# A two-layer attention encoder: block sums of the first seven-product group, an earlier weight split, and other banks for one set of transposes

## The chip, the cores and the metric

The kernel runs on one core of a Trainium2 chip. The metric is the device time in microseconds (us) of one execution. Before the change three runs took 1867.33, 1861.46 and 1866.14 us, with a median of 1866.14. A further execution was run under the hardware profiler; all rows below come from it.

## The reference, cut to what matters

The reference is an encoder trunk of two layers in float32, for 512 tokens of 1024 channels. Each layer does

```
h = RMSNorm(x);  four attention mixers, gated, merged
x = x + merged @ W_out                   (1024 x 1024)
hm = RMSNorm(x, mlp_norm_g)
u = square(relu(hm @ W_up))              (1024 x 4096)
x = x + u @ W_down                       (4096 x 1024)
```

The change touches the stretch from the second norm to the first quarter of `hm @ W_up`. It occurs once in each layer.

## The kernel before, in words

Matrix products must be close to float32, so every operand is split in two: `split` (lines 213 to 218) writes `hi`, a rounded copy made by ScalarE (line 215), and `lo`, the rest, made by VectorE (line 216, which waits for `hi`). A product of two operands is then three matmuls on TensorE: hi with hi, hi with lo, lo with hi.

**The order of work.** The program is written as one stream of instructions on tiles taken from pools. The tile framework then fixes one order for each engine at build time: it steps through a model of the run, and whenever an engine is free it takes, of the instructions that its model holds to be ready, an early one of the program. On the chip each engine goes through its fixed list and waits at every instruction for the data and buffers it needs. [...]

**Around the change, once in each layer.** `add_rows` (line 1097) adds `merged @ W_out` to the four token tiles `X[t]` of 128 tokens, and sums their squares on ScalarE (line 317). `norm` (line 324) then goes over the four tiles: eleven small VectorE instructions give the inverse root (`inverse`, lines 331 to 342), two scaled copies (line 349) write the normalised tile `both`, eight transposes on TensorE (line 222) bring it into two PSUM banks of four blocks each, `split` writes `h_hi` and `h_lo` from these banks, and ScalarE copies the banks to `h_raw` (line 361) for later sums. The transposes take their banks from the pool `sps`, which has four. Two more pools hold PSUM: `mm` with three banks, used by `add_rows` just before and by the products after, and `yps` with one.

The 4096 columns of `W_up` are done in four groups `j` of 1024, each of two halves `c` of 512.

- `j = 0, c = 0` is the plain group, `up_first` (line 1153). It loads 1024 x 512 weights as four blocks of 512 KB (`plain_blocks`, line 1136), splits each into `r_hi` and `r_lo` (pools of four buffers), and multiplies them first with tokens 0 to 255 (96 matmuls of 256 columns, which need the first two token tiles only) and then with tokens 256 to 511 (96 more).
- All other halves are done by `up` (line 1195), which needs seven products in place of eight for a 2 x 2 scheme of blocks. `row_sums` (line 1171) makes the sums of activation blocks from `h_raw`. The weight blocks are 512 x 256. One tile `t` starts as block (0,0); after its split for the first product, block (0,1) is added to it, then block (1,1), then block (1,0), with a product after each. Before the change such an addition is an accumulating DMA from HBM issued by GpSimd (`add_block`, line 1123). Another tile, `t3`, is block (0,1) plus block (1,1), added on VectorE (`merge`, line 1133). Each product is 24 matmuls (line 1215).
- From `j = 1` on, the products of `up` alternate with those of `add_product` (line 1325) for `W_down` of the group before.

Raw weights and the tiles `both` share the pool tag `r_raw` (eight buffers). All plain loads are issued by SyncE's queue (SP), in its own fixed order. Line 248 loads the weights of `add_rows`, line 1120 all blocks of `up`, line 321 the gain of the next norm.

Of the kernel before, what the change touches and what calls it, by code (L numbers as in the profile page):

```python
# [10 lines left out]
F32 = mybir.dt.float32  # L11
# [8 lines left out]
P = 128  # L20
S = 512
NT = S // P
D = 1024
# [15 lines left out]
class Weights:  # L39
# [7 lines left out]
    def add(self, layer, name, k0, kk, segs):  # L47
        n = sum(w for _, w in segs)
        off = self.size
        self.units.append((off, layer, name, k0, kk, tuple(segs), n))  # L50
        self.size += P * kk * n
        return off, n
# [45 lines left out]
class Plan:  # L98
# [12 lines left out]
    def take(self, what, n=1):  # L111
        self.free[what] -= n
        assert self.free[what] >= 0, what
# [51 lines left out]
class Net:  # L165
# [158 lines left out]
    def norm(self, pool, X, ms, g, tag="norm_h", bufs=2, keep=None):  # L324

        nc = self.nc
        hi = self.hp.tile([P, KD, S], F32R, name="h_hi", tag="h_hi")
        lo = self.hp.tile([P, KD, S], F32R, name="h_lo", tag="h_lo")
        stt = nc.vector.scalar_tensor_tensor

        def inverse(t):
            small = lambda name: pool.tile([P, 1], F32, name=name, tag=name, bufs=4)
            v, vh, y, w = small("norm_v"), small("norm_vh"), small("norm_y"), small("norm_w")
            nc.vector.tensor_scalar(v, ms[t][0], EPS, None, op0=ALU.add)
            for part in ms[t][1:]:
                nc.vector.tensor_tensor(v, v, part, op=ALU.add)
            nc.vector.tensor_scalar(y.bitcast(I32), v.bitcast(I32), -0.5, RSQRT_MAGIC, op0=ALU.mult, op1=ALU.add)
            nc.vector.tensor_scalar_mul(vh, v, -0.5)
            for _ in range(3):
                stt(w, y, y, vh, op0=ALU.mult, op1=ALU.mult)  # L340
                stt(y, w, 1.5, y, op0=ALU.add, op1=ALU.mult)
            return y

        y = inverse(0)
        for t in range(NT):
            both = pool.tile([P, 2, S], F32, name=tag, tag=tag, bufs=bufs)
            for half in range(2):
                cs = slice(half * S, half * S + S)
                stt(both[:, half, :], X[t][:, cs], y, g[:, cs], op0=ALU.mult, op1=ALU.mult)
            y = inverse(t + 1) if t + 1 < NT else None  # L350
            banks = []
            for half in range(2):
                ps = self.sps.tile([P, 4, P], F32, name="tp", tag="s")
                for j in range(4):
                    self.transpose(ps[:, j, :], both[:, half, j * P:(j + 1) * P])
                self.split(hi[:, half * 4:half * 4 + 4, t * P:(t + 1) * P],
                           lo[:, half * 4:half * 4 + 4, t * P:(t + 1) * P], ps)
                banks.append(ps)
            if keep is not None:
                for half, ps in enumerate(banks):  # L360
                    nc.scalar.copy(keep[half, t // 2][:, :, t % 2 * P:t % 2 * P + P], ps)
        return hi, lo
# [787 lines left out]

        return {(r, t): pool.tile([P, KD // 2, S // 2], F32, name=name, tag="u", bufs=NU) for r in range(2) for t in range(2)}

    def up_first(self, pool, layer, u):

        units = self.plain_blocks(pool, layer, "up", 0, 0)
        tiles = [self.mm.tile([P, S], F32, name="mm", tag="mm") for _ in range(3)]
        tiles.append(self.yps.tile([P, S], F32, name="mm_y", tag="y"))

        early, late = slice(0, S // 2), slice(S // 2, S)
        for f in range(4):  # L1160
            self.fm_group(tiles[f][:, early], self.hT, units, f * P, early)
            self.squared_relu(u[0, 0][:, f, :], tiles[f][:, early])
        for i in range(0, KD, 2):
            for f in range(4):
                for k, hi, lo in units[i:i + 2]:
                    self.mm3(tiles[f][:, late], (hi[:, f * P:f * P + P], lo[:, f * P:f * P + P]),
                             (self.hT[0][:, k, late], self.hT[1][:, k, late]), k == 0, k == KD - 1)
        for f in range(4):
            self.squared_relu(u[0, 1][:, f, :], tiles[f][:, late])
# [22 lines left out]
                self.split(hi[:, i, :], lo[:, i, :], sums[i][:, k, :])  # L1192
        return [own] + [[(hi[:, i, :], lo[:, i, :]) for hi, lo in rest] for i in range(3)]

    def up(self, pool, layer, c0, u, row, sums):


        nc = self.nc
        h, kh, n = S // 2, KD // 2, S // 2
        s1, s2, s3, s4 = sums  # L1200
        part = lambda ks, ts: [tuple(x[:, k, ts] for x in self.hT) for k in ks]
        x11, x12, x22 = (part(range(0, kh), slice(0, h)), part(range(kh, KD), slice(0, h)),
                         part(range(kh, KD), slice(h, S)))
        at = {(r, c): self.W.add(layer, "up", r * kh, kh, [(c0 + n * c, n)])[0] for r in range(2) for c in range(2)}
        load = lambda r, c: self.load_block(pool, at[r, c], kh, n)
        add = lambda raw, r, c: self.add_block(raw, at[r, c], kh, n)
        out = {(t, c): u[row, t][:, 2 * c:2 * c + 2, :] for t in range(2) for c in range(2)}
        bank = lambda: self.mm.tile([P, 2, h], F32, name="mm", tag="mm")

        def product(ps, left, raw, fresh):  # L1210
            right = self.split_block(pool, raw)
            for f in range(2):
                for k, (x, w) in enumerate(zip(left, right)):
                    for i, (a, b) in enumerate(((1, 0), (0, 0), (0, 1))):
                        nc.tensor.matmul(ps[:, f, :], w[a][:, f * P:(f + 1) * P], x[b], start=fresh and f + k + i == 0,  # L1215
                                         stop=k == kh - 1 and i == 2, skip_group_check=True)
                        self.pe(h)

        stt = nc.vector.tensor_tensor
        t = load(0, 0)  # L1220
        a = bank()
        product(a, x11, t, True)
        add(t, 0, 1)
        nc.scalar.copy(out[0, 0], a)
        yield
        c = bank()
        product(c, x12, load(1, 0), True)
        stt(out[0, 0], out[0, 0], c, op=ALU.add)
        self.squared_relu(out[0, 0], out[0, 0])
        yield  # L1230
# [1 line left out]
        product(b, s1, t, True)  # L1232
        add(t, 1, 1)
        nc.scalar.copy(out[1, 1], b)
        t3, w22 = load(0, 1), load(1, 1)
        self.merge(t3, w22)
        yield
        product(b, s4, w22, False)
# [114 lines left out]
    def run(self):  # L1353
# [14 lines left out]
        for layer in range(self.depth):  # L1368
            act = self.attention(layer)
            last = layer == self.depth - 1  # L1370
            with tc.tile_pool(name=f"mlp{layer}", bufs=1) as pool:
# [5 lines left out]
                mine = lambda k, t: tuple(x[:, k, t * P:(t + 1) * P] for x in act)  # L1377
                self.add_rows(pool, X, mine, layer, "out", 0, ms, self.merges)
                raw = self.blocks(pool, "h_raw")
                self.hT = self.norm(pool, X, ms, g, "r_raw", NRIGHT, raw)  # L1380
                if not last:
                    g = self.load_gain(pool, I["attn_norm_g"][layer + 1])
                prev = None
                for j in range(4):
                    u = self.blocks(pool, "u")
                    if j == 0:
                        self.up_first(pool, layer, u)
                        sums = self.row_sums(pool, raw)
                    for c in range(1 if j == 0 else 0, 2):
                        for i, _ in enumerate(self.up(pool, layer, j * D + c * S, u, c, sums)):  # L1390
                            if prev is not None and (i + c) % 2:
                                next(prev, None)
                    if j < 3:
                        prev = self.add_product(pool, X, u, layer, "down", j * KD)
# [89 lines left out]
```

## Time and profile before

| What | us |
|---|---|
| median of three runs | 1866.14 |
| lowest and highest run | 1861.46, 1867.33 |
| the profiled execution | 1864.41 |
| its span (first to last instruction) | 1862.6 |
| TensorE busy | 1772.7 (95%) |
| VectorE busy | 1320.9 (71%) |
| ScalarE busy | 1010.2 (54%) |
| GpSimd busy | 445.2 (24%) |
| mean granted TensorE clock | 0.979 of full speed |

PE stands for TensorE's matmuls, PEld for its weight loads, DVE for VectorE, ACT for ScalarE, POOL for GpSimd, SP for SyncE. PEclk is the clock that TensorE was granted, as a share of full speed; in a row that covers one level only it is either 1.00 (2.4 GHz) or 0.50 (1.2 GHz). In a timeline row the bracket at the end tells how long the engine sat idle before the row, and which instruction ended the wait. Matmuls overlap, so a matmul's duration is longer than the distance to the next one; some matmul records are missing from the trace. The stretch of the change is 588 to 662 us in the first layer and 1503 to 1578 us in the second.

### The profile page before, as it was taken

How to read it: one execution, taken by the hardware profiler on the slowest of the kernel's cores; microseconds unless marked ns; L12 is line 12 of the kernel's file. 1: busy time of each engine (PE TensorE's matmuls, PEld its weight loads, DVE VectorE, ACT ScalarE, POOL GpSimd, SP SyncE). 2: the span in 40 equal slices, each digit the busy share in tenths (PEclk: the TensorE clock that was granted, in tenths of full speed). 3: DMA queues.
4: the chain of work that ended last, by engine and by line, in shares of the span. 5: the costliest groups of instructions: out<-in, count | busy, mean ns of one | idle time of the engine just before them, and what ended most of it. 6: DMA issues, size and time to landing. Idle time of an engine off the chain costs nothing.

```text
span 1862.6 us, 28777 instructions
## 1 busy us (share of the span) xinstructions
PE 1772.7 (95%) x10256; PEld 1577.2 (85%) x10256; DVE 1320.9 (71%) x2645; ACT 1010.2 (54%) x1999; POOL 445.2 (24%) x1245
## 2 busy tenths in 40 slices
PE   6998999999998899999999989999999988999999
PEld 5897887787888899989888879887878888999897
DVE  6677866777655587878567878666876574877872
ACT  4565664455534566566436656645554355656561
POOL 2462254433110011111025504632412001111100
PEclk9998999999999899999999989999999989999999
DMA  4312122121334577878232221222222444878771
GB/s 163 116 53 69 58 80 84 43 69 55 90 91 164 159 179 190 183 194 191 79 105 97 76 60 52 78 72 68 66 66 78 154 145 104 191 192 194 172 178 46
DMA packets 71312, 209.76 MB, mean 113 GB/s; under 512 B 8704, under 2 KB 12288, under 8 KB 71168
## 3 DMA queue, kind: packets, MB, share of 16 engines
q1 hardware_dynamic: 59936, 167.02, 27.5%
q0 software_dynamic: 11232, 40.90, 13.1%
q8 instruction: 80, 1.31, 0.3%
q14 instruction: 64, 0.52, 0.1%
HBM read 203.70 MB, written 4.19 MB: 112 GB/s over the span
## 4 chain that ended last, share of the span: by engine, by line
PE 74%; DVE 8%; POOL 7%; issue 4%; DMA 3%; ACT 2%; SPq 0%; POOLq 0%; DVEq 0%; ACTq 0%
PE mm L1215 14%; PE mm L285 14%; PE mm L286 13%; PE mm L287 13%; PE u L1344 12%; PE tp L222 3%; DMA r_raw<-in_wflat 2%; POOL rs_w_qk L235 2%; PE s L615 2%; POOL rs_w_qk L236 1%; POOL rs_w_qk L237 1%; POOL rs_y_qk L238 1%; PE y L642 1%; PE y L641 1%; DVE w_lo L216 1%
## 5 line engine op out<-in xcount | busy, mean ns | idle before, releaser
L216 DVE TENSOR_TENSOR r_lo<-r_raw,r_hi 128x1024 fp32r<-128x1024 f32 x206 | 250.8, 1221 | 101.1 <-ACT r_hi L215 99.4
L215 ACT CAST r_hi<-r_raw 128x1024 fp32r<-128x1024 f32 x206 | 215.7, 1050 | 128.7 <-PE mm L1215 47.9
L216 DVE TENSOR_TENSOR w_lo<-w_raw,w_hi 128x768 fp32r<-128x768 f32 (+2 forms) x217 | 197.6, 917 | 56.7 <-ACT w_hi L215 54.8
L215 ACT CAST w_hi<-w_raw 128x768 fp32r<-128x768 f32 (+2 forms) x217 | 166.8, 779 | 119.7 <-PE mm L286 76.0
L1125 POOL DMA_DIRECT2D r_raw<-in_wflat x78 | 67.5, 865 | 645.2 <-DVE r_lo L216 641.4
L285 PE MATMUL mm<-h_hi,w_hi 128*128 128x512 f32 x544 | 217.9, 401 | 1.1 <-DVE sig L1040 1.0
L287 PE MATMUL mm<-h_hi,w_lo 128*128 128x512 f32 x544 | 214.4, 400 | 4.4 <-DVE w_lo L216 2.5
L286 PE MATMUL mm<-h_lo,w_hi 128*128 128x512 f32 x544 | 215.7, 397 | 0.0
L286 PE MATMUL mm<-w_lo,h_hi 128*128 128x384 f32 (+1 forms) x576 | 189.8, 331 | 3.4 <-DVE w_lo L216 3.3
L287 PE MATMUL mm<-w_hi,h_lo 128*128 128x384 f32 (+1 forms) x576 | 189.5, 330 | 2.6 <-DVE h_lo L216 2.6
L285 PE MATMUL mm<-w_hi,h_hi 128*128 128x384 f32 (+1 forms) x576 | 187.6, 332 | 1.0 <-ACT w_hi L215 0.5
L235 POOL TENSOR_TENSOR rs_w_qk<-rs_y_qk 128x4 f32<-128x4 f32 (+2 forms) x216 | 66.4, 307 | 415.6 <-DVE rs_y_qk L233 292.0
L1344 PE MATMUL u<-r_lo,l_hi 128*128 128x512 f32 x336 | 132.1, 393 | 0.2 <-DVE r_lo L216 0.2
L1215 PE MATMUL mm<-h_hi,r_lo 128*128 128x256 f32 x448 | 127.2, 284 | 4.8 <-DVE r_lo L216 4.8
L1344 PE MATMUL u<-r_hi,l_lo 128*128 128x512 f32 x336 | 131.6, 392 | 0.0
L1215 PE MATMUL mm<-h_lo,r_hi 128*128 128x256 f32 x448 | 128.2, 286 | 0.0
L1215 PE MATMUL mm<-h_hi,r_hi 128*128 128x256 f32 x448 | 128.0, 286 | 0.0
L1344 PE MATMUL u<-r_hi,l_hi 128*128 128x512 f32 x336 | 126.2, 390 | 0.0
L287 PEld LDWEIGHTS mm<-h_hi,w_lo 128*128 128x128 f32 x544 | 103.3, 190 | 26.8 <-DVE w_lo L216 4.0
L285 PEld LDWEIGHTS mm<-h_hi,w_hi 128*128 128x128 f32 x544 | 103.8, 191 | 23.5 <-DVE sig L1040 2.9
L286 PEld LDWEIGHTS mm<-h_lo,w_hi 128*128 128x128 f32 x544 | 103.5, 190 | 20.5
L286 PEld LDWEIGHTS mm<-w_lo,h_hi 128*128 128x128 f32 x576 | 109.8, 191 | 5.7 <-DVE w_lo L216 4.6
(226 smaller groups left out, 4745.9 us busy)
## 6 DMA issues: line engine op xcount, KB each, us to landing
r_raw<-in_wflat SPq DMA_DIRECT2D x128, 512.0 KB, 4.6
w_raw<-in_wflat SPq DMA_DIRECT2D x168, 384.0 KB, 3.2
r_raw<-in_wflat POOLq DMA_DIRECT2D x78, 512.0 KB, 5.7
w_raw<-in_wflat SPq DMA_DIRECT2D x48, 256.0 KB, 2.6
x<-in_x SPq DMA_DIRECT2D x8, 512.0 KB, 5.6
d_full<-in_mask_d SPq DMA_DIRECT2D x8, 448.0 KB, 4.1
x_save<-x SPq DMA_DIRECT2D x4, 512.0 KB, 2.6
x<-x_save SPq DMA_DIRECT2D x4, 512.0 KB, 4.8
```

The costliest lines, as they stand in the source:

```text
L215: self.nc.scalar.copy(hi, src)
L216: self.nc.vector.tensor_tensor(lo, src, hi.bitcast(F32), op=ALU.subtract)
L222: self.nc.tensor.transpose(out, in_, self.ident_r if short else self.ident)
L235: eng.tensor_tensor(w, y, y, op=ALU.mult)
L236: eng.tensor_tensor(w, w, v, op=ALU.mult)
L285: nc.tensor.matmul(ps, st[0], mv[0], start=first, stop=False)
L286: nc.tensor.matmul(ps, st[0], mv[1], start=False, stop=False)
L287: nc.tensor.matmul(ps, st[1], mv[0], start=False, stop=last)
L615: self.nc.tensor.matmul(ps, q[:, qc], k[:, kc], start=i == 0, stop=i == len(ks) - 1)
L1125: self.nc.gpsimd.dma_start(raw, self.source(off, kk, n), accum_op=ALU.add)
L1215: nc.tensor.matmul(ps[:, f, :], w[a][:, f * P:(f + 1) * P], x[b], start=fresh and f + k + i == 0, stop=k == kh - 1 and i == 2, skip_group_ ...
L1344: nc.tensor.matmul(ps[q], a[:, k, toks], b, start=fresh and k + i == 0, stop=k == len(w) - 1 and i == 2, skip_group_check=True)
```

## The change

Three edits.

1. In the norm ahead of the MLP (the one with `keep`), the transposes of the third token tile (`t == 2`) take their two banks from the pool `mm` in place of `sps`.
2. `plain_blocks` for the plain group (four loads, four splits) stands in the program ahead of the norm, behind `add_rows`. Its result is handed to `up_first`.
3. In the first group (`j == 0`) `up` is called with `alone`: it loads its four weight blocks at once and keeps them, and the three additions to `t` are made by VectorE from the kept blocks (`merge`), where they were accumulating DMAs. The other groups do as before.

```diff
--- before.py
+++ after.py
@@ -350,7 +350,10 @@
             y = inverse(t + 1) if t + 1 < NT else None
             banks = []
             for half in range(2):
-                ps = self.sps.tile([P, 4, P], F32, name="tp", tag="s")
+                if keep is not None and t == 2:
+                    ps = self.mm.tile([P, 4, P], F32, name="tp_mm", tag="mm")
+                else:
+                    ps = self.sps.tile([P, 4, P], F32, name="tp", tag="s")
                 for j in range(4):
                     self.transpose(ps[:, j, :], both[:, half, j * P:(j + 1) * P])
                 self.split(hi[:, half * 4:half * 4 + 4, t * P:(t + 1) * P],
@@ -1150,9 +1153,8 @@
 
         return {(r, t): pool.tile([P, KD // 2, S // 2], F32, name=name, tag="u", bufs=NU) for r in range(2) for t in range(2)}
 
-    def up_first(self, pool, layer, u):
-
-        units = self.plain_blocks(pool, layer, "up", 0, 0)
+    def up_first(self, units, u):
+
         tiles = [self.mm.tile([P, S], F32, name="mm", tag="mm") for _ in range(3)]
         tiles.append(self.yps.tile([P, S], F32, name="mm_y", tag="y"))
 
@@ -1192,7 +1194,8 @@
                 self.split(hi[:, i, :], lo[:, i, :], sums[i][:, k, :])
         return [own] + [[(hi[:, i, :], lo[:, i, :]) for hi, lo in rest] for i in range(3)]
 
-    def up(self, pool, layer, c0, u, row, sums):
+    def up(self, pool, layer, c0, u, row, sums, alone=False):
+
 
 
         nc = self.nc
@@ -1203,7 +1206,15 @@
                          part(range(kh, KD), slice(h, S)))
         at = {(r, c): self.W.add(layer, "up", r * kh, kh, [(c0 + n * c, n)])[0] for r in range(2) for c in range(2)}
         load = lambda r, c: self.load_block(pool, at[r, c], kh, n)
-        add = lambda raw, r, c: self.add_block(raw, at[r, c], kh, n)
+        held = {(r, c): load(r, c) for r, c in ((0, 0), (1, 0), (0, 1), (1, 1))} if alone else {}
+        take = lambda r, c: held[r, c] if alone else load(r, c)
+
+        def add(raw, r, c):
+            if alone:
+                self.merge(raw, held[r, c])
+            else:
+                self.add_block(raw, at[r, c], kh, n)
+
         out = {(t, c): u[row, t][:, 2 * c:2 * c + 2, :] for t in range(2) for c in range(2)}
         bank = lambda: self.mm.tile([P, 2, h], F32, name="mm", tag="mm")
 
@@ -1217,14 +1228,14 @@
                         self.pe(h)
 
         stt = nc.vector.tensor_tensor
-        t = load(0, 0)
+        t = take(0, 0)
         a = bank()
         product(a, x11, t, True)
         add(t, 0, 1)
         nc.scalar.copy(out[0, 0], a)
         yield
         c = bank()
-        product(c, x12, load(1, 0), True)
+        product(c, x12, take(1, 0), True)
         stt(out[0, 0], out[0, 0], c, op=ALU.add)
         self.squared_relu(out[0, 0], out[0, 0])
         yield
@@ -1232,7 +1243,7 @@
         product(b, s1, t, True)
         add(t, 1, 1)
         nc.scalar.copy(out[1, 1], b)
-        t3, w22 = load(0, 1), load(1, 1)
+        t3, w22 = take(0, 1), take(1, 1)
         self.merge(t3, w22)
         yield
         product(b, s4, w22, False)
@@ -1377,6 +1388,7 @@
                 mine = lambda k, t: tuple(x[:, k, t * P:(t + 1) * P] for x in act)
                 self.add_rows(pool, X, mine, layer, "out", 0, ms, self.merges)
                 raw = self.blocks(pool, "h_raw")
+                units = self.plain_blocks(pool, layer, "up", 0, 0)
                 self.hT = self.norm(pool, X, ms, g, "r_raw", NRIGHT, raw)
                 if not last:
                     g = self.load_gain(pool, I["attn_norm_g"][layer + 1])
@@ -1384,10 +1396,10 @@
                 for j in range(4):
                     u = self.blocks(pool, "u")
                     if j == 0:
-                        self.up_first(pool, layer, u)
+                        self.up_first(units, u)
                         sums = self.row_sums(pool, raw)
                     for c in range(1 if j == 0 else 0, 2):
-                        for i, _ in enumerate(self.up(pool, layer, j * D + c * S, u, c, sums)):
+                        for i, _ in enumerate(self.up(pool, layer, j * D + c * S, u, c, sums, j == 0)):
                             if prev is not None and (i + c) % 2:
                                 next(prev, None)
                     if j < 3:
```

## Rows read from the trace of the kernel before

**Rows 1.** The profile's page: busy by engine, chain of waits by engine, accumulating loads
```profile
PE 1772.7 (95%) x10256; PEld 1577.2 (85%) x10256; DVE 1320.9 (71%) x2645; ACT 1010.2 (54%) x1999; POOL 445.2 (24%) x1245
...
PE 74%; DVE 8%; POOL 7%; issue 4%; DMA 3%; ACT 2%; SPq 0%; POOLq 0%; DVEq 0%; ACTq 0%
...
r_raw<-in_wflat POOLq DMA_DIRECT2D x78, 512.0 KB, 5.7
```

**Rows 2.** Busy time by stretch: PE, PEld, DVE, ACT, POOL; PEclk, DMA share, GB/s
```profile
597.00:608.10 11.10, 5.10 (x33) 4.02 (x31) 9.24 (x24) 8.40 (x17) 0.00 (x0) 0.77 0.11 24
608.10:613.20 5.10, 5.10 (x24) 5.10 (x25) 5.00 (x5) 4.25 (x6) 0.00 (x0) 0.50 0.98 349
646.70:650.40 3.70, 3.70 (x17) 3.70 (x18) 2.21 (x2) 1.26 (x3) 0.85 (x1) 0.50 0.53 70
662.00:680.00 18.00, 18.00 (x119) 16.46 (x118) 15.24 (x16) 13.27 (x17) 2.70 (x4) 1.00 0.75 179
1569.70:1574.40 4.70, 4.70 (x22) 4.70 (x23) 2.91 (x3) 2.31 (x3) 0.86 (x1) 0.50 0.83 193
```

**Rows 3.** Timeline of TensorE: start, duration, form, count, idle before and releaser
```profile
600.74 1.33 PE L222 MATMUL tp<-ident,r_raw 128*128 128x128 f32 x8 [1.89 <-ACT h_raw L361]
605.40 1.94 PE L222 MATMUL tp<-ident,r_raw 128*128 128x128 f32 x8 [3.33 <-DVE r_raw L349]
608.10 0.58 PE L285 MATMUL mm<-h_hi,r_hi 128*128 128x256 f32 x1 [0.77 <-ACT r_hi L215]
...
633.29 0.28 PE L1215 MATMUL mm<-h_hi,r_lo 128*128 128x256 f32 x1
633.40 0.28 PE L1215 MATMUL mm<-h_hi,r_hi 128*128 128x256 f32 x1
...
646.69 0.58 PE L1215 MATMUL mm<-w_hi,r_lo 128*128 128x256 f32 x1 [4.71 <-DVE r_lo L216]
655.97 0.38 PE L1215 MATMUL mm<-h_hi,r_lo 128*128 128x256 f32 x1 [1.49 <-DVE r_lo L216]
...
1560.46 0.39 PE L1215 MATMUL mm<-w_hi,r_lo 128*128 128x256 f32 x1 [3.42 <-DVE r_lo L216]
1569.70 0.58 PE L1215 MATMUL mm<-h_hi,r_lo 128*128 128x256 f32 x1 [3.28 <-DVE r_lo L216]
```

**Rows 4.** Timeline of GpSimd's accumulating DMAs, first of the group
```profile
629.30 1.02 POOL L1125 DMA_DIRECT2D r_raw<-in_wflat  x1 [110.67 <-DVE r_lo L216]
```

**Rows 5.** Timeline of ScalarE at the first of these additions
```profile
632.09 0.37 ACT L1146 ACTIVATE u<-mm 128x256 f32<-128x256 f32 x1
636.39 1.05 ACT L215 CAST r_hi<-r_raw 128x1024 fp32r<-128x1024 f32 x1 [3.94 <-DMA r_raw<-in_wflat]
637.34 0.41 ACT L1147 ACTIVATE u<-u 128x256 f32<-128x256 f32 x1
```

**Rows 6.** Timeline of VectorE in the norm and the plain group
```profile
598.05 1.41 DVE L349 SCALAR_TENSOR_TENSOR r_raw<-x,norm_y,norm_g 128x512 f32<-128x512 f32 x2
...
600.05 1.88 DVE L216 TENSOR_TENSOR h_lo<-tp,h_hi 128x512 fp32r<-128x512 f32 x3
...
604.50 1.42 DVE L349 SCALAR_TENSOR_TENSOR r_raw<-x,norm_y,norm_g 128x512 f32<-128x512 f32 x2
...
610.01 2.36 DVE L216 TENSOR_TENSOR r_lo<-r_raw,r_hi 128x1024 fp32r<-128x1024 f32 x2
...
618.97 1.22 DVE L1134 TENSOR_TENSOR r_raw<-r_raw 128x1024 f32<-128x1024 f32 x1
```

**Rows 7.** Busy time by stretch, columns as in rows 2: norm, then seven products
```profile
588.30:605.90 17.60, 12.37 (x78) 11.65 (x77) 15.91 (x54) 8.67 (x20) 0.00 (x0) 0.92 0.22 87
633.30:658.00 24.70, 18.51 (x139) 18.10 (x138) 10.72 (x10) 12.49 (x20) 2.59 (x3) 0.86 0.55 137
```

**Rows 8.** The tile of raw weights, 580 to 600 us: issues, landing times
```profile
L1120 SPq DMA_DIRECT2D r_raw<-in_wflat x4: 424/428/493, 584.7 to 586.1; - x4
...
DMA to landing us min/median/max: 4.4/6.3/7.5
```

## The prediction

> **What bounds the kernel now.** I read the page first: TensorE is busy for 95% of the span and carries 74% of the chain of waits [rows 1]. So I looked for stretches in which it waits or runs at the low clock, first by stretches, then row by row. Right behind the change, from 662 us, TensorE is busy for 18.00 of 18.00 us at PEclk 1.00, with VectorE at 15.24 [rows 2]: time won ahead of that point is not taken back by TensorE there. What can be won is what TensorE loses inside the stretch.
>
> In the norm it waits three times [rows 3]: 1.89 us for a bank of `sps`, ended by ScalarE's copy to `h_raw`; 3.33 us for the scaled copy of the fourth token tile; 0.77 us for the first `r_hi` of the plain group. That is 5.99 us. Between 597 and 608.1 it is busy for 5.10 of 11.10 us, and the clock falls: PEclk is 0.77 on average there and 0.50 throughout 608.1 to 613.2, where TensorE is busy without a break [rows 2].
>
> In the first seven products it waits 4.71 and 1.49 us in the first layer, and 3.42 and 3.28 us in the second, each time for an `r_lo` [rows 3]. What is late lies two steps ahead. GpSimd issues the accumulating DMA at 629.30 [rows 4]; ScalarE, idle for 3.94 us, starts on the sum at 636.39 [rows 5]. After 646.7 the clock is 0.50 for 3.70 us of work, in the second layer after 1569.7 for 4.70 us [rows 2].
>
> **The additions on VectorE.** Removed: three accumulating DMAs per layer, each with about 1.0 us of issue on GpSimd and typically 5.7 us to land [rows 1, 4]. For the first one, issue to start of the split is 636.39 - 629.30 = 7.09 us. Added: three `merge` instructions of 1.22 us, the same form as the one at 618.97 [rows 6]. The chain of tile `t` is then merge 1.22, `r_hi` 1.05 [rows 5], `r_lo` 1.18 (two take 2.36 [rows 6]); with some 0.1 to 0.2 us at each handover (estimate from the idle times between such rows) about 3.8 us per addition. Three make 11.4 us. A matmul starts every 0.11 to 0.12 us [rows 3], so with 0.12 a product of 24 takes 2.9 us, and the seven take 20.2 us, so TensorE hides the chain. What I expect late next is TensorE itself. Behind a waiting merge on VectorE stand the other `r_lo` and the additions of products to `u`; VectorE is busy for only 10.72 of 24.70 us there [rows 7], and 3.66 us more fit. The four blocks are loaded once each in both versions; they come from plain loads of SP, and one of them, block (1,0), holds its buffer until its late addition. I cost that at nothing, since loads stand in advance; without that cover it is one landing, 4.4 to 7.5 us [rows 8], per layer.
>
> Gain in the first layer: 4.71 + 1.49 idle, and half of 3.70 us, 1.85, for the clock: 8.05 us. Second layer: 3.42 + 3.28 + 2.35 = 9.05 us. Together 17.1 us. I leave 0.5 us of new small waits in each layer and take 16; bounds 6 (one landing lost in each layer is 5.7, so 17.1 - 11.4 = 5.7) and 17.1.
>
> The Trainium skill (DMA: Bandwidth & Descriptors, "SDMA does more than copy") says that the DMA engines can add two streams on their way, so that no compute engine does the addition. By that reading the edit only adds 3.66 us of VectorE work per layer, 7.3 us in all if VectorE were the bound. Rows 5 and 7 say otherwise here: the transfer is waited for, and VectorE has room.
>
> **The weight split ahead of the norm.** Nothing is added; four `r_hi` (1.05 us each) and four `r_lo` (1.22 us each, two in a row 2.36, so 1.14 apart [rows 6]) move. Their loads are issued by SP at 584.7 to 586.1 already and land 4.4 to 7.5 us later [rows 8], by 593.6 at the latest, but the first `r_hi` ends at 608 only [rows 3], so it starts near 607: its place is behind most of the norm. ScalarE is busy for 8.67 of 17.60 us in the norm, so 4.2 us fit there at no cost. VectorE is busy for 15.91 of these 17.60 us [rows 7]: 1.69 us are free, and 4 x 1.14 = 4.56 are to be placed. So up to 2.9 us of the norm's VectorE work is pushed back. Against this stands what the early split allows: the plain group's first 96 matmuls need only the first two token tiles, whose last `h_lo` ends at 600.05 + 1.88 = 601.93 [rows 6]. With `r_hi` and `r_lo` there, TensorE can run them in the 3.33 us in which it now waits for the fourth tile. This needs the order of TensorE's list to put some of them ahead of the fourth tile's transposes. Lists are filled by what is ready, and now the split will be, so I take that as likely.
>
> **The third tile's banks.** The 1.89 us wait goes as such: the additions of `add_rows` that read the banks of `mm` stand ahead of this tile's norm on VectorE. The two scaled copies of this tile end at 598.05 + 1.41 = 599.46 [rows 6], so its transposes start about 1.3 us earlier than 600.74. Alone this is worth at most 1.89 us per layer and nothing if VectorE sets the fourth tile's time anyway. It costs something where the plain group then waits for the two borrowed banks until they are copied to `h_raw`; the third bank of `mm` and the one of `yps` are free before, which is work for 2 x 24 matmuls, so I cost this at nothing, at most 1 us.
>
> **The norm's sum, per layer.** From the start of the plain group's matmuls there are 192 of them and 8 transposes, 200 x 0.12 = 24.0 us of TensorE work at full clock. The start is 601.9 if no split is in VectorE's way, and 601.9 + 2.9 = 604.8 if all are; I take the middle, 603.3, so the end would be 627.3, against 633.29 now [rows 3]: 6.0 us. The low clock may still come, since TensorE still waits about 3.4 us in two pieces between 598.9 and 603.3. In the trace it cost half of the 1.94 us transposes and half of 5.10 us, 3.5 us in all; I charge 2. That leaves 4.0 us per layer, 8 for both. Bounds: 7.4 without low clock and without push-back, and -2.1 with both in full and no overtaking (0.77 gained, 2.9 lost).
>
> Sum: 16 + 8 = 24 us. Against the profiled execution, 1864.4 - 24 = 1840.4 us; the median of the runs shown is 1.7 us above it, so 1842 us.
>
> **The rivals.**
> - *No overtaking.* The fourth tile's transposes stay ahead of all matmuls of the plain group. For it: in the list of now no matmul stands in that wait of 3.33 us [rows 3]. Against it: none could, with the first `r_hi` done at 608. The norm then gives 0 to 1 us per layer: 16 + 1 = 17 us, about 1849, down to 1854 with VectorE's push-back.
> - *The additions change one wait for another.* The merges or their blocks come late: 5.7 us of the group's 17.1 remains, the norm gives 0 to 4: 1856 to 1862. For it: the blocks are loaded behind the gain of the next norm in SP's order in the first layer. Against it: that gain waits for the last scaled copy, which ends at 604.50 + 1.42 = 605.9 [rows 6], and 7.5 us of landing after that is 613.4, while the products start near 627.
> - *The early weights hold up VectorE.* This one ends slower. Lists are worked through in order: ScalarE's square at 637.34 stands behind the sum that landed late, though the rows ahead of it had long ended [rows 5]. If the four `r_lo` stand ahead of the norm's first instructions and weights land late, the whole norm moves by that time, each us costing one us in each layer. With weights landed by 593.6, the fourth `r_lo` ends near 596 and the norm is pushed by some 4 to 5 us, which with the low clock in full (3.5) eats the norm's 7.4 us and no more. To end slower, the push must pass 7.4 - 3.5 + 8.5 = 12.4 us per layer; with 15 us it would be 1866.1 + 2 x 2.6, about 1871. The Trainium skill (TensorE: Matmul & The Clock Gate, "Architectural detail") calls the queues of ScalarE and VectorE strictly first in, first out; the row at 637.34 agrees.
>
> **How the numbers follow.** Forecast 0.62, 1834 to 1849; no overtaking 0.20, 1849 to 1854; changed waits 0.13, 1856 to 1862; held up 0.05, about 1871. The range that leaves out no more than two in ten is 1833 to 1855. A measurement of this kernel tells about 0.3%, 5.6 us, from no change. Forecast, no overtaking and half of the third case are faster: 0.88; the other half 0.07 within; slower 0.05.
>
> **What would show it.** Right: no wait over 1 us of TensorE in the first seven products, and their 20 us at PEclk 1.00; matmuls of line 285 between the third and the fourth tile's transposes; the first product near 629 rather than 633.3. Wrong: a wait of TensorE there that ends on `r_lo` behind a merge, or the fourth tile's scaled copy later than 609. The forecast fails if the time after 662 us does not simply move forward by what was won.

## The result, and the profile after

The changed kernel takes 1838.38 us (median of 4 runs, 1838.09 to 1839.71) beside 1866.74 us for the kernel before in the same batch (1861.46 to 1868.85): a ratio of 0.9854, 95% interval [0.9832, 0.9875], or 28 us less. A second batch gave 1839.28 and 0.9861 [0.9844, 0.9877]. The two profiled executions, which the comparison below rests on, took 1864.41 and 1839.71 us, so 24.7 us of the difference can be placed.

To place it, the time from the program's first matmul to its last is cut at the first matmuls of the stages: the output product of `add_rows`, the first transpose of the MLP's norm, the first of the seven products, the first matmul of W_down. Lengths in us:

| stage | before | after | difference |
|---|---|---|---|
| from the first matmul to the first output product | 541.36 | 542.51 | +1.15 |
| output product, layers 1 / 2 | 47.39 / 46.97 | 48.02 / 51.43 | +0.63 / +4.46 |
| norm and plain group, 1 / 2 | 36.34 / 36.11 | 27.99 / 27.98 | -8.35 / -8.13 |
| seven products, 1 / 2 | 34.17 / 35.57 | 26.95 / 27.78 | -7.22 / -7.79 |
| the work between, W_down of layer 1 to the output product of layer 2 | 797.81 | 797.79 | -0.02 |
| from W_down of layer 2 to the last matmul | 274.31 | 274.83 | +0.52 |

They add up to -24.75 us. What was won ahead of the long stretch of 798 us is kept there to 0.02 us.

The profile's page answers to [rows 1]: TensorE's busy time fell by 9.7 us with the same 10256 matmuls, so they ran less at the low clock, and GpSimd's share of the chain fell from 7% to 5%.

```profile
PE 1763.0 (96%) x10256; PEld 1568.4 (85%) x10256; DVE 1326.6 (72%) x2651; ACT 1010.2 (55%) x1999; POOL 441.3 (24%) x1239
...
PE 77%; DVE 8%; POOL 5%; DMA 3%; issue 3%; ACT 2%; SPq 1%; DVEq 0%; POOLq 0%; ACTq 0%
```

Busy time by stretch (columns as in [rows 2]) of the kernel after: the norm, the plain group (two rows), the seven products of the first layer, and then two stretches of the second layer's output product.

```profile
597.00:608.00 11.00, 10.00 (x78) 9.30 (x77) 9.61 (x30) 6.86 (x16) 0.00 (x0) 1.00 0.00 1
608.00:613.20 5.20, 5.20 (x47) 5.20 (x46) 1.37 (x2) 2.89 (x7) 0.00 (x0) 1.00 0.84 247
613.20:626.50 13.30, 13.30 (x114) 13.30 (x113) 12.99 (x20) 10.77 (x26) 0.00 (x0) 1.00 0.25 102
626.50:655.00 28.50, 27.44 (x226) 27.04 (x225) 21.76 (x21) 20.18 (x30) 3.62 (x4) 1.00 0.49 125
1463.00:1476.00 13.00, 11.91 (x76) 11.59 (x74) 8.13 (x14) 8.15 (x15) 0.00 (x0) 1.00 0.95 359
1476.60:1482.40 5.80, 5.22 (x20) 4.90 (x21) 2.65 (x6) 0.90 (x3) 0.00 (x0) 0.71 0.22 70
```

From 597 to 655 us PEclk is 1.00 throughout, where it was 0.77 and 0.50 [rows 2]. TensorE's own timeline shows which waits are left. The norm has one, of 0.98 us; the fourth tile's transposes (two rows of x4) stand among matmuls of L285 to L287; the seven products wait once in each layer, 1.06 and 1.88 us. And there is a wait that was not there before, at 1476.65.

```profile
598.78 1.91 PE L222 MATMUL tp<-ident,r_raw 128*128 128x128 f32 x16
600.70 1.32 PE L222 MATMUL tp_mm<-ident,r_raw 128*128 128x128 f32 x8
601.77 0.36 PE L285 MATMUL mm<-h_hi,r_hi 128*128 128x256 f32 x1
...
603.23 0.39 PE L286 MATMUL mm<-h_lo,r_hi 128*128 128x256 f32 x1 [0.98 <-DVE h_lo L216]
...
609.98 0.60 PE L222 MATMUL tp<-ident,r_raw 128*128 128x128 f32 x4
610.33 0.36 PE L287 MATMUL mm<-h_hi,r_lo 128*128 128x256 f32 x1
...
610.66 0.60 PE L222 MATMUL tp<-ident,r_raw 128*128 128x128 f32 x4
...
642.22 0.39 PE L1226 MATMUL mm<-h_hi,r_lo 128*128 128x256 f32 x1 [1.06 <-DVE r_lo L216]
...
1476.65 0.80 PE L285 MATMUL mm<-w_hi,m_hi 128*128 128x384 f32 x3 [1.74 <-ACT w_hi L215]
1477.98 0.69 PE L286 MATMUL mm<-w_lo,m_hi 128*128 128x384 f32 x1 [0.53 <-DVE w_lo L216]
...
1547.20 0.39 PE L1226 MATMUL mm<-h_hi,r_lo 128*128 128x256 f32 x1 [1.88 <-DVE r_lo L216]
```

VectorE, in the same form: the four `r_lo` of the plain group run from 569.24 to 574.3, in the output product, some 24 us ahead of the norm's first scaled copy; the fourth scaled copy starts at 606.34; then come the merges of the seven products. The last two merges shown, at 639.80 and 1544.79, wait for a DMA and stand ahead of an `r_lo`.

```profile
569.24 5.09 DVE L216 TENSOR_TENSOR r_lo<-r_raw,r_hi 128x1024 fp32r<-128x1024 f32 x4 [1.19 <-ACT r_hi L215]
...
593.53 1.41 DVE L349 SCALAR_TENSOR_TENSOR r_raw<-x,norm_y,norm_g 128x512 f32<-128x512 f32 x2
...
606.34 1.42 DVE L349 SCALAR_TENSOR_TENSOR r_raw<-x,norm_y,norm_g 128x512 f32<-128x512 f32 x2
...
626.71 2.48 DVE L1137 TENSOR_TENSOR r_raw<-r_raw 128x1024 f32<-128x1024 f32 x2
...
638.33 1.23 DVE L216 TENSOR_TENSOR r_lo<-r_raw,r_hi 128x1024 fp32r<-128x1024 f32 x1 [1.11 <-ACT r_hi L215]
639.80 1.23 DVE L1137 TENSOR_TENSOR r_raw<-r_raw 128x1024 f32<-128x1024 f32 x1 [0.25 <-DMA r_raw<-in_wflat]
640.94 1.22 DVE L216 TENSOR_TENSOR r_lo<-r_raw,r_hi 128x1024 fp32r<-128x1024 f32 x1
...
1544.79 1.23 DVE L1137 TENSOR_TENSOR r_raw<-r_raw 128x1024 f32<-128x1024 f32 x1 [1.07 <-DMA r_raw<-in_wflat]
```

SP's queue says why. The loads of the plain blocks (L1123) are now issued at 560, ahead of the eight output weights (L248), which wait for buffers for most of their 22.84 us; before, they stood behind these, at 584.7 [rows 8].

```profile
560.02 1.92 SPq L1123 DMA_DIRECT2D r_raw<-in_wflat  x4
564.83 22.84 SPq L248 DMA_DIRECT2D w_raw<-in_wflat  x8
```

In the second layer the same order costs time. The issues between 1460 and 1480 us of the kernel after, with the median time to landing in the last column:

```profile
r_raw<-in_wflat SPq DMA_DIRECT2D x4, 512.0 KB, 11.2
w_raw<-in_wflat SPq DMA_DIRECT2D x4, 384.0 KB, 9.8
```

and of the kernel before, 1470 to 1490 us:

```profile
w_raw<-in_wflat SPq DMA_DIRECT2D x5, 384.0 KB, 4.1
```

The output weights take 5.7 us longer to land. ScalarE's timeline after: `r_hi` after `r_hi` waits for its block, and `w_hi` stands behind the fourth.

```profile
1470.89 1.05 ACT L215 CAST r_hi<-r_raw 128x1024 fp32r<-128x1024 f32 x1 [2.20 <-DMA r_raw<-in_wflat]
...
1474.75 1.04 ACT L215 CAST r_hi<-r_raw 128x1024 fp32r<-128x1024 f32 x1 [0.23 <-DMA r_raw<-in_wflat]
1475.77 0.83 ACT L215 CAST w_hi<-w_raw 128x768 fp32r<-128x768 f32 x1
```

### The profile page after: what moved, and what is told of

Its sections match the earlier page's. It is cut to its first block, busy times and chain, and to the rows that moved or that the text cites. A ratio compares the mean times of both kernels' runs of the same rounds, so it can differ in the third digit from the quotient of the medians.

```text
span 1837.9 us, 28747 instructions
## 1 busy us (share of the span) xinstructions
PE 1763.0 (96%) x10256; PEld 1568.4 (85%) x10256; DVE 1326.6 (72%) x2651; ACT 1010.2 (55%) x1999; POOL 441.3 (24%) x1239
## 4 chain that ended last, share of the span: by engine, by line
PE 77%; DVE 8%; POOL 5%; DMA 3%; issue 3%; ACT 2%; SPq 1%; DVEq 0%; POOLq 0%; ACTq 0%
PE mm L285 14%; PE mm L286 14%; PE mm L287 14%; PE mm L1226 14%; PE u L1355 12%; PE tp L222 4%; PE s L618 2%; DMA r_raw<-in_wflat 2%; POOL rs_w_qk L235 2%; PE y L645 1%; DVE w_lo L216 1%; PE y L644 1%; POOL rs_w_qk L236 1%; POOL rs_w_qk L237 1%; POOL rs_y_qk L238 1%
## 5 line engine op out<-in xcount | busy, mean ns | idle before, releaser
L287 PE MATMUL mm<-h_hi,w_lo 128*128 128x512 f32 x544 | 214.6, 400 | 4.9 <-DVE w_lo L216 2.5
L285 PE MATMUL mm<-h_hi,w_hi 128*128 128x512 f32 x544 | 218.1, 402 | 0.6 <-DVE sig L1043 0.5
L1128 POOL DMA_DIRECT2D r_raw<-in_wflat x72 | 62.5, 868 | 624.4 <-DVE r_lo L216 372.8
L287 PE MATMUL mm<-w_hi,h_lo 128*128 128x384 f32 (+1 forms) x576 | 190.2, 331 | 2.7 <-DVE h_lo L216 2.7
L285 PE MATMUL mm<-w_hi,h_hi 128*128 128x384 f32 (+1 forms) x576 | 188.2, 333 | 0.8 <-ACT w_hi L215 0.5
L287 PEld LDWEIGHTS mm<-h_hi,w_lo 128*128 128x128 f32 x544 | 103.6, 190 | 27.6 <-DVE w_lo L216 4.0
L285 PEld LDWEIGHTS mm<-h_hi,w_hi 128*128 128x128 f32 x544 | 103.8, 191 | 22.8 <-DVE sig L1043 1.9
```

Of the source, the lines that this page charges most:

```text
L285: nc.tensor.matmul(ps, st[0], mv[0], start=first, stop=False)
L287: nc.tensor.matmul(ps, st[1], mv[0], start=False, stop=last)
L1128: self.nc.gpsimd.dma_start(raw, self.source(off, kk, n), accum_op=ALU.add)
```

## The experiments

Each diff is cut to the lines that carry the edit.

**e1_only_sums** is the kernel before with the additions on VectorE alone.

```diff
-        add = lambda raw, r, c: self.add_block(raw, at[r, c], kh, n)
+        held = {...four loads...} if alone else {}
+        def add(raw, r, c):
+            if alone: self.merge(raw, held[r, c])
+            else: self.add_block(raw, at[r, c], kh, n)
...
```

> Only the additions on VectorE; plain weights and banks as before. Theory A (the edits act in different places and add up): the norm keeps its three waits, 5.99 us per layer, and the low clock after them; the seven products lose their waits. In the changed kernel's trace the stretch behind the first product is 7.2 and 7.3 us shorter, so about 14.5 us less than before: 1852 us, 1850 to 1854. Theory B (the additions are hidden only because the kept blocks are loaded some 20 us earlier behind an early split): waits of several us stay in the products, 1858 us or more.

1850.92 us, ratio 0.9921 [0.9907, 0.9935]. The norm's waits stand as they were, and of the products' four waits one of 0.76 us is left. The group fell from 34.17 and 35.57 to 25.81 and 26.65 us: 8.4 and 8.9 us won, beside the 8.05 and 9.05 of the prediction before its residual. Timeline of TensorE:

```profile
604.78 1.94 PE L222 MATMUL tp<-ident,r_raw 128*128 128x128 f32 x8 [3.33 <-DVE r_raw L349]
...
1555.84 0.38 PE L1223 MATMUL mm<-h_hi,r_lo 128*128 128x256 f32 x1 [0.76 <-DVE r_lo L216]
```

**e2_only_split** is the kernel before with the split ahead of the norm alone.

```diff
+                units = self.plain_blocks(pool, layer, "up", 0, 0)
                 self.hT = self.norm(pool, X, ms, g, "r_raw", NRIGHT, raw)
...
-                        self.up_first(pool, layer, u)
+                        self.up_first(units, u)
```

> Only the weight split ahead of the norm; additions by accumulating DMA and banks as before. Theory A: the stretch from the first transposes to the first product is about 8 us shorter per layer less up to 1.9 us for the banks; the hold-up of the output weights (0.6 us in the first layer, 4.4 us in the second) comes with it: 1855 to 1859 us. Theory B (the accumulating chain, not TensorE, ends the first group, so an earlier start is waited away): waits in the products grow by as much, 1864 to 1868 us.

1849.39 us, ratio 0.9913 [0.9900, 0.9926]: better than either theory. Norm and plain group take 28.18 us in both layers, 8 us less each; theory A had up to 1.9 us less than that for the banks, and the prediction 4. The second layer's output product grew to 49.58 us, so 2.61 of the 4.46 us found there come with this edit alone. And the products gained 2.87 and 1.43 us without any change to the additions. Timeline of TensorE: 4.71 [rows 3] became 2.13 us, and the wait behind it kept its 1.49. The last row, by stretch, shows the clock behind the two waits of the output product.

```profile
636.95 0.39 PE L1223 MATMUL mm<-w_hi,r_lo 128*128 128x256 f32 x1 [2.13 <-DVE r_lo L216]
...
1479.95 0.80 PE L285 MATMUL mm<-w_hi,m_hi 128*128 128x384 f32 x3 [1.48 <-ACT w_hi L215]
1481.27 0.45 PE L286 MATMUL mm<-w_lo,m_hi 128*128 128x384 f32 x1 [0.51 <-DVE w_lo L216]
...
1481.50:1485.00 3.50, 3.50 (x21) 3.50 (x21) 1.80 (x5) 1.39 (x5) 0.00 (x0) 1.00 0.30 112
```

The first wait shrank because the chain of additions starts earlier beside the products. The first accumulating DMA is issued at 621.30, and the split of its sum starts at 626.82, 0.71 us behind the first product (626.11). Before, that split started 3.10 us behind it (636.39 [rows 5] for 633.29 [rows 3]). These 2.39 us are nearly the 2.58 us by which the wait shrank.

**e3_no_banks** is the changed kernel with the third tile's transposes in the banks they had.

```diff
-                if keep is not None and t == 2:
-                    ps = self.mm.tile([P, 4, P], F32, name="tp_mm", tag="mm")
-                else:
-                    ps = self.sps.tile([P, 4, P], F32, name="tp", tag="s")
+                ps = self.sps.tile([P, 4, P], F32, name="tp", tag="s")
```

> The changed kernel without the other banks for the third tile. Theory A: TensorE has ready matmuls of the plain group while it would wait for a bank, so at most 1 us is lost per layer: 1838 to 1840 us. Theory B (the bank wait of 1.89 us stays on the path): 1842 us or more, with a wait of TensorE ended by the copy to h_raw.

1837.60 us, ratio 0.9851 [0.9839, 0.9864]: no difference. The wait for the bank, 1.89 us before, is 0.32 us now even in the old banks, since matmuls of the plain group stand ahead of these transposes. Timeline of TensorE:

```profile
601.43 0.62 PE L285 MATMUL mm<-h_hi,r_hi 128*128 128x256 f32 x3 [0.84 <-ACT h_hi L215]
602.48 0.66 PE L222 MATMUL tp<-ident,r_raw 128*128 128x128 f32 x4 [0.32 <-ACT h_raw L361]
```

**e4_split_mid** moves the loads and the split of the plain blocks into the norm, between its first and second token tile.

```diff
-                units = self.plain_blocks(pool, layer, "up", 0, 0)
-                self.hT = self.norm(pool, X, ms, g, "r_raw", NRIGHT, raw)
+                units = []
+                self.hT = self.norm(pool, X, ms, g, "r_raw", NRIGHT, raw,
+                                    lambda: units.extend(self.plain_blocks(pool, layer, "up", 0, 0)))
```

> The changed kernel with the four loads and splits of the plain group made in the program between the first and the second token tile of the norm, so that SP loads them behind the output weights. Theory A (the loss in the output product of the second layer, 4.4 us with its low clock, comes from the early splits standing ahead of a weight split on ScalarE): that loss goes, the first add 0.6 too; the splits now share VectorE with the norm and push it by up to 2.9 us per layer, of which the plain group's matmuls hide most: 1833 to 1838 us. Theory B (the loss is a matter of memory traffic or of chance, and VectorE's push is on the path): 1840 to 1846 us.

1841.28 us, ratio 0.9868 [0.9854, 0.9882]. The output product is back at 47.32 and 46.94 us, and the norm is longer, 31.31 and 30.29 us: here is the push-back that the prediction charged. The fourth scaled copy stands behind the `r_lo` in VectorE's queue, and TensorE waits twice at the start of its plain group. Timeline of VectorE (the first of the four `r_lo`, and the fourth tile's copy):

```profile
595.50 1.23 DVE L217 TENSOR_TENSOR r_lo<-r_raw,r_hi 128x1024 fp32r<-128x1024 f32 x1
...
609.19 1.41 DVE L352 SCALAR_TENSOR_TENSOR r_raw<-x,norm_y,norm_g 128x512 f32<-128x512 f32 x2
```

Timeline of TensorE, and by stretch:

```profile
600.74 0.39 PE L286 MATMUL mm_y<-h_hi,r_hi 128*128 128x256 f32 x1 [1.79 <-ACT h_hi L216]
602.32 0.39 PE L287 MATMUL mm_y<-h_lo,r_hi 128*128 128x256 f32 x1 [1.19 <-DVE h_lo L217]
...
602.40:606.00 3.60, 3.60 (x19) 3.60 (x20) 3.60 (x11) 1.67 (x4) 0.00 (x0) 0.57 0.95 379
```

What this kernel won at one place it lost at the other; another 3.4 us went in the work between the layers' stages (801.19 us), which I cannot place. The time is in theory B's range and the output product came back as theory A had it. Both the early transfers and the early splits are gone here, so this kernel does not tell which of them cost the time.

**e5_half_half** loads and splits two blocks ahead of the norm and two between its first tiles; **e6_gain_late** is the changed kernel with the load of the norm's gain moved behind `add_rows`; **e7_half_late** is both. The diff is that of e5.

```diff
-                units = self.plain_blocks(pool, layer, "up", 0, 0)
-                self.hT = self.norm(pool, X, ms, g, "r_raw", NRIGHT, raw)
+                units = self.plain_blocks(pool, layer, "up", 0, 0, (0, 4))
+                self.hT = self.norm(pool, X, ms, g, "r_raw", NRIGHT, raw,
+                                    lambda: units.extend(self.plain_blocks(pool, layer, "up", 0, 0, (4, KD))))
```

> The changed kernel with two of the four plain blocks ahead of the norm and two between its first and second token tile. Theory A (in the second layer the output weights land late behind the plain group's 2 MB in the DMA queues, 9.7 to 10.4 us after issue where it was 4.1 to 4.5, and TensorE waits 1.74 and 0.53 us and falls to the low clock): with 1 MB ahead they land some 2.6 us earlier, the 4.4 us are mostly won back; two late splits take 2.3 us of VectorE in the norm, of which about 1.7 are free: 1833 to 1836 us. Theory B (it is the order on ScalarE, or chance): 1838 to 1842 us.

> The changed kernel with the norm's gain (512 KB) loaded behind add_rows in the program, so that it stands behind the plain group's blocks in SP's list. Theory A (memory traffic): blocks land 1.3 us earlier or the output weights are no earlier at all, since the same bytes stay ahead of them; no change, 1837 to 1839 us, the waits in the second layer still 1.5 to 2.5 us. Theory B (ScalarE's order): the splits end about 1.3 us earlier and the weight split behind them too, 1835 to 1837 us.

> As the one with two blocks ahead and two in the norm, and the norm's gain behind the first two blocks. Theory A: as that one or up to 1 us faster, 1832 to 1836 us. Theory B: 1838 to 1842 us.

1837.83, 1836.19 and 1836.74 us, ratios 0.9857 [0.9836, 0.9877], 0.9851 [0.9828, 0.9873] and 0.9847 [0.9829, 0.9865]: none differs from the changed kernel, so their times do not tell the theories apart. e5 shortens the second output product to 47.71 us and lengthens the norm to 28.84 and 30.18. In e6 the wait stays, 1.94 us for 1.74, so the 512 KB of the gain are not what makes the weights late. e7 has the output product at 46.97 with the norm at 28.84 and 30.20.

**e8_sums_gpsimd** is the changed kernel with the three additions on GpSimd, from the same kept blocks.

```diff
-                self.merge(raw, held[r, c])
+                nc.gpsimd.tensor_tensor(raw, raw, held[r, c], op=ALU.add)
```

> The changed kernel with the three additions to tile t made by GpSimd instead of VectorE, from the same kept blocks. GpSimd takes 1.54 us for 128x512 elements, so about 3 us for one of these, twice and a half VectorE's 1.22. Theory A (what counts is that the chain of three additions with their splits stays below the 20 us of the seven products): the chain is about 3 x (3.0 + 1.05 + 1.2 + 0.2) = 16.4 us, still hidden: 1837 to 1841 us. Theory B (the short addition on VectorE itself is what wins): 3 x 1.8 us later in each layer, 1845 us or more, with waits on r_lo in the products.

1845.07 us, ratio 0.9891 [0.9874, 0.9907]. One addition takes 3.29 to 4.39 us where VectorE takes 1.22, and from one to the next are 6.9 and 5.7 us. Three such steps no longer hide behind the products: TensorE waits 1.75 and 0.50 us in the first layer and 1.76 and 2.04 us in the second, the stages take 29.93 and 31.47 us, and the time is where theory B had it. So the length of the chain counts, and it is not enough that the DMA's landing is out of it. Timeline of GpSimd, and of TensorE:

```profile
624.11 4.39 POOL L1214 TENSOR_TENSOR r_raw<-r_raw 128x1024 f32<-128x1024 f32 x1 [104.97 <-DVE r_lo L216]
630.98 3.32 POOL L1214 TENSOR_TENSOR r_raw<-r_raw 128x1024 f32<-128x1024 f32 x1 [2.47 <-DVE r_lo L216]
636.71 3.29 POOL L1214 TENSOR_TENSOR r_raw<-r_raw 128x1024 f32<-128x1024 f32 x1 [2.42 <-DVE r_lo L216]
...
636.69 0.39 PE L1226 MATMUL mm<-w_hi,r_lo 128*128 128x256 f32 x1 [1.75 <-DVE r_lo L216]
```

**e9_load_early** keeps the loads ahead of the norm and puts only the splits between its first two tiles; **e10_change_again** is the changed kernel beside it.

```diff
-                units = self.plain_blocks(pool, layer, "up", 0, 0)
-                self.hT = self.norm(pool, X, ms, g, "r_raw", NRIGHT, raw)
+                units = []
+                raws = self.plain_raws(pool, layer, "up", 0, 0)
+                self.hT = self.norm(pool, X, ms, g, "r_raw", NRIGHT, raw,
+                                    lambda: units.extend(self.plain_splits(pool, raws)))
```

> The changed kernel with the four plain blocks still loaded ahead of the norm, but split between its first and second token tile, as in e4_split_mid, whose loads stood there too. Theory A (what holds TensorE up in the output product is the order on ScalarE: the r_hi stand ahead of w_hi and wait for their block): the output product lasts 47.3 and 47.0 us as in e4_split_mid, with the loads early; time near 1841. Theory B (the 2 MB of plain blocks make the output weights land late, whoever splits them): it lasts 48.0 and 51.4 us as in the changed kernel, and with the norm of e4_split_mid (31.3 and 30.3 us) the time is 1841 + 0.7 + 4.5, near 1846. Whichever holds, the landing of the output weights issued near 1466 should stay near 10 us, since the same transfers are in flight.

> The changed kernel itself, beside the kernel before in five rounds on the chip of e9_load_early. Both theories: 1838 us and the same stage lengths as in its first profile (output product 48.0 and 51.4, norm 28.0 and 28.0, seven products 27.0 and 27.8 us). It tells how far the lengths of one profile can be trusted: if one differs by over 0.5 us from the first, smaller differences between the other kernels say nothing.

e9 took 1838.00 us, ratio 0.9854 [0.9839, 0.9868], with the stages of the changed kernel: output product 47.96 and 51.51, norm 27.97 twice. It tells the theories apart no further, because the edit moved nothing: VectorE's timeline has the splits at 568 to 573 us again, though the program writes them behind the norm's first tile.

```profile
568.02 5.08 DVE L217 TENSOR_TENSOR r_lo<-r_raw,r_hi 128x1024 fp32r<-128x1024 f32 x4 [1.24 <-ACT r_hi L216]
```

What it does show, beside e4, is that here the place of the loads in the program, and not that of the splits, decided when the blocks were split. e10 repeated every stage of the changed kernel to 0.3 us but the last, which differs by 0.4.

**e11_idle_loads** is e4_split_mid with four loads ahead of the norm that nothing reads.

```diff
                 units = []
+                for k in range(0, KD, 2):
+                    self.load_block(pool, k * P * S, 2, S)
                 self.hT = self.norm(...)
```

> e4_split_mid (the plain blocks loaded and split in the norm) with four more loads of 512 KB ahead of the norm in each layer, into buffers that no instruction reads; so the transfers of the changed kernel are there, 2 MB per layer ahead of the output weights, without its r_hi on ScalarE and r_lo on VectorE at that place. Theory B (the transfers make the output weights land late and TensorE wait): the output product of the second layer lasts near 51 us rather than 46.9, that of the first near 48, and the weights issued near 1466 land after about 10 us rather than 3 to 5; time 1841.3 + 0.7 + 4.4, near 1846. Theory A (the order on ScalarE: r_hi ahead of w_hi): 47.3 and 46.9 us, time near 1841, with landings that may be longer but end ahead of their w_hi.

1843.14 us, ratio 0.9867 [0.9847, 0.9887]. No `r_hi` stands ahead of `w_hi` here, and yet it waits 6.92 us for its weights, and TensorE for it. Timelines of ScalarE and TensorE:

```profile
1478.20 0.83 ACT L216 CAST w_hi<-w_raw 128x768 fp32r<-128x768 f32 x1 [6.92 <-DMA w_raw<-in_wflat]
...
1479.09 0.79 PE L286 MATMUL mm<-w_hi,m_hi 128*128 128x384 f32 x3 [1.22 <-ACT w_hi L216]
1480.08 0.44 PE L287 MATMUL mm<-w_lo,m_hi 128*128 128x384 f32 x1 [0.21 <-DVE w_lo L217]
```

Median landings, 1460 to 1480 us of this kernel, are those of the changed one:

```profile
r_raw<-in_wflat SPq DMA_DIRECT2D x4, 512.0 KB, 10.9
w_raw<-in_wflat SPq DMA_DIRECT2D x3, 384.0 KB, 9.6
```

The output product takes 47.66 and 49.28 us, so the transfers alone make 0.34 of the 0.70 and 2.34 of the 4.49 us by which the changed kernel stands above e4. Theory B has the mechanism and half of the size. The other half of the second layer is a little more waiting, 1.74 + 0.53 against 1.22 + 0.21 us (0.84 us), and the clock: the changed kernel ran the 5.8 us from 1476.6 at PEclk 0.71, some 1.7 us lost (an estimate, 0.29 of 5.8), while e11 kept 1.00. e2 helps to tell the two apart. It has `r_hi` ahead of `w_hi` like the changed kernel and waits 1.48 + 0.51 us, but its clock stayed at 1.00, and its stage takes 49.58 us, 0.30 more than e11's. So the order in ScalarE's and VectorE's queues added about 0.3 us there, and most of the 1.85 us from e2 to the changed kernel is the clock. That rests on one profile of each kernel; e10 repeats the 0.71.

## Why the forecast of 1842 us held, point by point

**The total.** It was 24 us off the profiled execution and 24.7 came, but by terms that missed on both sides: additions 15.0 where 16 was taken, norm 16.5 where 8 was taken, output product -5.1 where nothing stood, and -1.7 for the small differences at both ends of the table. The errors cancelled, so that the total came out this close is luck.

**The additions on VectorE: right.** The chain per addition is short enough for the products to hide it: after the change the waits 4.71 and 1.49, and 3.42 and 3.28 us [rows 3], are one of 1.06 and one of 1.88 us, somewhat more than the 0.5 us per layer that was left for them. e1 shows the gain without the other edits: 8.4 and 8.9 us, where 8.05 and 9.05 were worked out.

The wait that is left is the prediction's own sign of being wrong, a wait that ends on an `r_lo` behind a merge, at a small size. The first four merges are the three additions and `t3` of this half; the fifth, at 639.80, is by that count the one for `t3` of the next half, and its block lands late. VectorE was done with the `r_lo` ahead of it at 638.33 + 1.23 = 639.56 and started the next `r_lo` at 640.94, 1.38 us later, which covers TensorE's 1.06. In the second layer the merge waits 1.07 us for its block, and TensorE 1.88. So the kept blocks cost nothing, as the prediction had it, and no merge of theirs waits for a DMA; a block of the next half, which it did not price, cost this wait. The alternative in which additions change one wait for another thus holds for about 1 and 2 us on VectorE, and for more with the slower adder (e8). Its upper bound of 1862 us does not come out of its own terms: 1866.1 - 5.7 is 1860.4.

**The split ahead of the norm: mechanism right, size wrong.** The overtaking came as expected, and the first product starts at 626.76 where near 629 was named, although the norm begins 1.8 us later than before (633.29 - 36.34 = 596.95, and 598.78). The step that failed is the placing of the split: "Their loads are issued by SP at 584.7 to 586.1 already" was read from the trace of before [rows 8] and kept for the kernel after. The line moved, and its four DMAs with it, ahead of the eight output weights, to 560.02. So `r_lo` ran in the output product, and the charge for VectorE's push-back, 1.4 us between 0 and 2.9, was 0. The 2 us charged for the low clock were 0 too: the stage lost its waits, 5.99 - 0.98 = 5.01 us, and 8.35 - 5.01 = 3.34 us of low clock. With both charges at 0 the prediction's sum gives 7.4 us, its upper bound, and 8.35 and 8.13 came. The term that was too small there is the start: the plain group begins at 601.77, 3.0 us behind the norm's first transposes, where the sum had 601.9 - 596.95 = 5.0, since its first matmuls need `h_hi` and not yet `h_lo`; 0.98 us of that went into the wait for `h_lo`. The 24.0 us of work behind the start came out as charged (626.76 - 601.77 - 0.98 = 24.0). That the push-back is real where the split does fall into the norm is e4: the stage is 3.3 and 2.3 us longer than in the changed kernel.

**What was not in the sum.** The prediction counted the moved step's instructions and not what its transfers stand in front of. The blocks land one behind the other (the first and the fourth `r_hi`, each waiting for its block, start 3.86 us apart), and the output weights behind them: four blocks of 512 KB are 2 MB, at the 359 GB/s of the row 1463 to 1476 5.8 us, and the output weights take 9.8 - 4.1 = 5.7 us longer to land. The first layer hides most of it (+0.63); in the second (+4.46) the transfers alone cost 2.3 us (e11), and most of the rest is the clock behind the waits. The rival of early weights that hold up an engine thus had the right resource in the wrong place: it was looked for in the norm's VectorE, and stands in the output product. The Trainium skill (DMA: Bandwidth & Descriptors, "Queues, rings and completion order") says that all DMAs issued by SP share one row of rings, and that each DMA engine takes their descriptors in the order of the ring; e11, where loads that nobody reads delay the weights behind them, agrees.

**The banks: right.** At most 1.89 us and nothing if other work fills the place; e3 measures nothing.

**What is left open.** Stages of 540 to 543 us ahead of the first edit differ between kernels by up to 2.4 us (540.28 in e5, 542.71 in e7) and repeat within one (542.51 and 542.56 for the changed kernel); no run looked into that. Putting the additions of all groups on VectorE was not tried. Why the clock fell behind the waits of the changed kernel and not behind those of e2 stays open.

## What to carry to other kernels

When a line of the program moves, read its DMAs' new place in the issuing queue before its instructions' new place on the engines: here the load decided when the work ran, and what was loaded behind it. Here a transfer that was summed in flight stood on the path with its whole landing, 7.1 us from issue to the split for 1.2 us of VectorE's work; VectorE had room, and the plain addition won. A forecast that comes true in its total should still be checked by stage.

## What the runs showed of the hardware that was not expected

The same addition of 128x1024 fp32 took 1.22 us on VectorE and 3.29 to 4.39 us on GpSimd (e8).

A short wait cost time again in the clock in some places and not in others. In the kernel before, TensorE waited 3.42 us [rows 3] and the work behind it ran at PEclk 1.00, by stretch:

```profile
1560.50:1566.40 5.90, 5.90 (x48) 5.72 (x48) 2.18 (x2) 1.43 (x4) 0.86 (x1) 1.00 0.71 138
```

Nine us later it waited 3.28 us and the work behind that ran at 0.50 [rows 2]. In the output product of the second layer, waits of 1.48 and 0.51 us were followed by 1.00 in e2, and waits of 1.53 and 0.51 us at the same place by 0.61 from 1481 to 1485 us in e8. So in this case the clock's part of a wait was not to be told from the wait's length.
